# The Mamba-2 mixer of a two-layer trunk: silu by tanh, decays group by group, and an order kept on four engines

## The chip, the cores and the metric

The kernel runs on one core of a Trainium2 chip. The metric is device microseconds of one execution. TensorE is called PE in the profile, VectorE DVE, ScalarE ACT, GpSimd POOL and SyncE SP.

## The reference

A trunk of two layers works on x, 256 tokens of width 1024, in float32. Each layer adds half a SwiGLU FFN, a token mixer, a cross-attention into 256 memory tokens and another half FFN, each behind an rmsnorm. Layer 0's mixer is a differential attention; layer 1's, which this change is about, is a Mamba-2 SSD mixer with 8 groups of 4 heads, state 128 and chunks of 128 tokens:

```
z, xbc, dt = jnp.split(h @ w_in, ...)
xbc = silu(causal_depthwise_conv(xbc, conv_w, conv_b))       # 4 taps
xs, Bm, Cm = jnp.split(xbc, ...)
dt = softplus(dt + dt_bias)
y = ssd_chunked_scan(xs * dt, dt * -exp(A_log), Bm, Cm)
#   cb = C B^T;  decay = exp(a_cs[l] - a_cs[s]), lower triangle
#   y_diag = (cb * decay) x;  states = B^T (decay_to_end x);  y_off = exp(a_cs) C state
y = (y + D_skip * xs) * silu(z)
y = rmsnorm over each group of 256, * gnorm
out = y @ w_out
```

## The kernel before

**Products.** Every weight is loaded by SP into one of four 1 MB tiles (L161) and cut into *granules* of 128x1024. A granule is split into a rounded part `whi`, cast by ACT (L183), and a remainder `wlo`, subtracted by DVE (L184); four pairs of such tiles exist (pool `hp`). Each product is three matmuls, hi by hi, hi by lo and lo by hi (`mm3`, L221 to L223). `use` (L197) asks, when a granule comes up, for the splits up to `AHEAD` = 2 granules beyond it.

**Order.** The work is a list of units, each some granules and a function. `Pipe` (L108 to L140) keeps a time that advances with the matmuls emitted; a step given to `pipe.after(us, f)` is emitted when that time is reached, so the numbers in such calls set the order in which instructions are written. `run_units` (L202) then decides which engines keep that order: in the mixer only TensorE does, and a scheduler orders the other engines.

**The mixer** (`ssd`, L901). After the key and value products for the memory tokens (`mk`) and the unit `zdt` (the first half of z's first pair, and dt), `sums` makes the cumulative sums `acs` and `out_of_psum` writes them to a DRAM tile `scr`. `spread(g)` loads them back for group g, broadcast over the partitions, as tiles `E`, one per chunk (L997); `decay` turns such a tile into differences with four relus on ACT (L1011) and `decay2` into decays with one exp per chunk (L1015). Four pairs of groups follow, each with units b, c, xs (two) and z. The channels b, c and xs go through `conv`: a first tap on ACT (L1026), three taps on DVE for each half j (L1033), and silu with the bias on ACT, one 128x256 half at a time (L1038). z goes through silu on ACT straight from PSUM (L1081). For each group, TensorE then turns b (`tb`, L1087) and multiplies c by b (`pcb`, L1092); ACT copies `bn` (L1096); DVE masks `pcb` into `cbm` (L1098) and multiplies it into the two `E` tiles (L1100). TensorE turns xs (`tx`, L1107), ACT copies it (`xn`, L1111), and GpSimd makes `xd`, `xe` and the skip part `xn` (L1115 to L1119). TensorE computes the state (`pst`, L1128), the diagonal part (`py`, L1133) and the part from the first chunk's state (`pof`, L1147); DVE adds and gates (`y`, L1140 to L1156, with `yo`); ACT sums the squares (L1161) and scales (L1165), DVE prepares `msq` (L313); TensorE turns y (`ty`, L1176), and ACT and DVE split it into `y_hi` and `y_lo` (L306, L308). After the last pair the 16 granules of `out` follow.

Of the kernel before, what the change touches and what calls it, by code (L numbers as in the profile page):

```python
# [7 lines left out]
F32 = mybir.dt.float32  # L8
# [15 lines left out]
AHEAD = 2  # L24
# [33 lines left out]
def trunk(ctx, tc, a, out):  # L58
# [129 lines left out]
    done = [0]  # L188

# [6 lines left out]
    def use(gr):  # L196

        for g in gr:
            ready(g.at + AHEAD + 1)
            yield g  # L200

    def run_units():  # L202
# [698 lines left out]
    def ssd(norm, nxt, kv):  # L901
# [8 lines left out]
        dte = const.tile([P, 32], F32, name="dte")  # L910
        E = {}
# [29 lines left out]
        def dt_steps(pd):  # L941
# [15 lines left out]
            def third():  # L957
# [9 lines left out]
                v.scalar_tensor_tensor(av, dt, -1.0, nega.unsqueeze(1).broadcast_to(d32), op0=ALU.mult, op1=ALU.mult)  # L967
                pipe.after(5.0, sums)
            pipe.after(1.0, second)

        def sums():
# [9 lines left out]
            def out_of_psum():  # L981
# [35 lines left out]
        def conv(ps, ch, name, wait):  # L1017
# [18 lines left out]
            def silu():  # L1036
                for j in range(2):
                    nc.scalar.activation(o[:, j, :], o[:, j, :], AF.Silu, bias=cb_[:, ch[j]:ch[j] + 1])  # L1038
# [26 lines left out]
        def group(g):  # L1065
# [3 lines left out]
            def xs_fin(ps):  # L1069
                s["xs"] = conv(ps, (2 * g, 2 * g + 1), "xs", 6.5)  # L1070
                if g == 0:
                    s["zs"] = held.pop()
                    pipe.after(6.5, lambda: nc.scalar.activation(s["zs"], s["zs"], AF.Silu))
                pipe.after(9.5, turn_x)

            def z_fin(ps):
                zs = v2(slot("zs"))

                def go():
                    for t in range(2):  # L1080
                        nc.scalar.activation(zs[:, t, :], ps[t], AF.Silu)  # L1081
# [3 lines left out]
            def cross():  # L1085
# [8 lines left out]
                def go():  # L1094
                    s["bn"] = work("bn", P)
                    nc.scalar.copy(s["bn"], tb[:, 0:P])  # L1096
                    cbm = work("cbm", S).rearrange("p (c l) -> p c l", c=2)
                    v.tensor_tensor(cbm, pcb[:, 0:2, :], triu.unsqueeze(1).broadcast_to([P, 2, P]), op=ALU.mult)  # L1098
# [4 lines left out]
            def turn_x():  # L1103
# [5 lines left out]
                def go():  # L1109
# [34 lines left out]
            def state():  # L1144
# [7 lines left out]
                def gate():  # L1152
                    yo = work("yo", S)
                    v.tensor_tensor(r4(yo), r4(pof), b4(eacs[:, hs]), op=ALU.mult)
# [13 lines left out]
                pipe.after(evac + 7.0, lambda: rc.append(rpow(ss[:, 0:2], 1.0 / 256, 2, "yrc")))  # L1168
# [26 lines left out]
        for i in range(4):  # L1195
# [161 lines left out]
```

## Time and profile before

| | before |
|---|---|
| median of 3 runs | 1319.79 us (1319.79 to 1320.98) |
| profiled execution | 1322.33 us, span 1320.6 us |
| granted TensorE clock, mean | 0.994 |
| HBM read | 229.77 MB, 175 GB/s over the span |
| TensorE chain share of the span | 88% |

A page of the profile gives busy times by engine, the chain of work that ended last, and the costliest groups of instructions, named by the line and by output <- input. The trace behind it answers questions on windows of time, on what an engine waited for, and on the single instructions.

### The profile page before, as it was taken

How to read it: one execution, taken by the hardware profiler on the slowest of the kernel's cores; microseconds unless marked ns; L12 is line 12 of the kernel's file. 1: busy time of each engine (PE TensorE's matmuls, PEld its weight loads, DVE VectorE, ACT ScalarE, POOL GpSimd, SP SyncE). 2: the span in 40 equal slices, each digit the busy share in tenths (PEclk: the TensorE clock that was granted, in tenths of full speed). 3: DMA queues.
4: the chain of work that ended last, by engine and by line, in shares of the span. 5: the costliest groups of instructions: out<-in, count | busy, mean ns of one | idle time of the engine just before them, and what ended most of it. 6: DMA issues, size and time to landing. Idle time of an engine off the chain costs nothing.

```text
span 1320.6 us, 17832 instructions
## 1 busy us (share of the span) xinstructions
PE 1302.2 (99%) x6995; PEld 1118.0 (85%) x6995; DVE 808.7 (61%) x1178; ACT 739.8 (56%) x1208; POOL 65.2 (5%) x68
## 2 busy tenths in 40 slices
PE   9999999999999999999999999989999999999998
PEld 6888888788988888888888889889998898888887
DVE  5655457876666555555556456657985775655554
ACT  6456444585455544444445446899765664644532
POOL 1000002200000000000000000022311000000000
PEclk9999999999999999999999999889999999999999
DMA  8565555435445554656555546743544444555651
GB/s 303 191 223 173 194 178 189 129 127 166 163 150 162 190 190 128 231 184 203 181 190 186 183 156 219 222 158 128 163 157 159 160 160 157 189 181 175 207 176 49
DMA packets 134631, 232.02 MB, mean 176 GB/s; under 512 B 5737, under 2 KB 34066, under 8 KB 134546
## 3 DMA queue, kind: packets, MB, share of 16 engines
q1 hardware_dynamic: 133648, 229.75, 52.7%
q8 instruction: 55, 0.90, 0.3%
q10 hardware_dynamic: 738, 0.59, 0.1%
q0 software_dynamic: 160, 0.52, 0.1%
q14 instruction: 30, 0.25, 0.0%
HBM read 229.77 MB, written 1.08 MB: 175 GB/s over the span
## 4 chain that ended last, share of the span: by engine, by line
PE 88%; ACT 6%; DVE 2%; DMA 2%; issue 1%; POOL 1%; SPq 0%; POOLq 0%; ACTq 0%; DVEq 0%
PE out L221 7%; PE out L223 7%; PE out L222 7%; PE up L222 5%; PE up L223 5%; PE up L221 5%; PE gate L223 5%; PE gate L221 5%; PE gate L222 5%; PE htp L603 1%; PE fin L222 1%; PE fin L221 1%; PE fin L223 1%; ACT whi L183 1%; PE xq L222 1%
## 5 line engine op out<-in xcount | busy, mean ns | idle before, releaser
L184 DVE TENSOR_TENSOR wlo<-w,whi 128x1024 fp32r<-128x1024 f32 (+2 forms) x446 | 523.9, 1180 | 416.9 <-ACT whi L183 415.2
L183 ACT CAST whi<-w 128x1024 fp32r<-128x1024 f32 (+1 forms) x448 | 448.1, 1007 | 467.2 <-PE out L223 146.6
L222 PE MATMUL up<-wlo,xh 128*128 128x512 f32 x320 | 124.7, 390 | 1.1 <-DVE wlo L184 1.1
L221 PE MATMUL up<-whi,xh 128*128 128x512 f32 x320 | 124.6, 389 | 0.0
L223 PE MATMUL up<-whi,xl 128*128 128x512 f32 x320 | 124.5, 389 | 0.0
L221 PE MATMUL gate<-whi,xh 128*128 128x512 f32 x312 | 123.2, 395 | 0.0
L223 PE MATMUL gate<-whi,xl 128*128 128x512 f32 x312 | 121.6, 390 | 0.0
L222 PE MATMUL gate<-wlo,xh 128*128 128x512 f32 x312 | 121.5, 389 | 0.0
L221 PE MATMUL out<-whi,hid_hi 128*128 128x512 f32 x264 | 103.5, 392 | 0.0
L223 PE MATMUL out<-whi,hid_lo 128*128 128x512 f32 x264 | 102.8, 389 | 0.0
L222 PE MATMUL out<-wlo,hid_hi 128*128 128x512 f32 x264 | 102.7, 389 | 0.0
L222 PEld LDWEIGHTS up<-wlo,xh 128*128 128x128 f32 x320 | 60.1, 188 | 14.3 <-DVE wlo L184 1.9
L221 PEld LDWEIGHTS up<-whi,xh 128*128 128x128 f32 x320 | 60.1, 188 | 12.8 <-ACT whi L183 0.4
L223 PEld LDWEIGHTS up<-whi,xl 128*128 128x128 f32 x320 | 60.1, 188 | 12.4
L223 PEld LDWEIGHTS gate<-whi,xl 128*128 128x128 f32 x312 | 58.5, 188 | 12.3
L221 PEld LDWEIGHTS gate<-whi,xh 128*128 128x128 f32 x312 | 58.6, 188 | 11.5
L222 PEld LDWEIGHTS gate<-wlo,xh 128*128 128x128 f32 x312 | 58.6, 188 | 11.5
L223 PEld LDWEIGHTS out<-whi,hid_lo 128*128 128x128 f32 x264 | 49.6, 188 | 10.4
L222 PEld LDWEIGHTS out<-wlo,hid_hi 128*128 128x128 f32 x264 | 49.6, 188 | 10.1
L221 PEld LDWEIGHTS out<-whi,hid_hi 128*128 128x128 f32 x264 | 49.6, 188 | 9.9
L315 POOL TENSOR_TENSOR rcol<-msq,neghalf 128x2 f32<-128x2 f32 x8 | 5.6, 697 | 691.2 <-DVE msq L313 691.2
L221 PE MATMUL xs<-xh,whi 128*128 128x256 f32 x128 | 38.0, 297 | 0.2 <-ACT whi L183 0.2
(354 smaller groups left out, 2741.7 us busy)
## 6 DMA issues: line engine op xcount, KB each, us to landing
w<-in_ffn_w_up_dram SPq DMA_DIRECT2D x40, 1024.0 KB, 5.1
w<-in_ffn_w_down_dram SPq DMA_DIRECT2D x40, 1024.0 KB, 5.1
w<-in_ffn_w_gate_dram SPq DMA_DIRECT2D x38, 1024.0 KB, 5.1
w<-in_ssd_w_in_dram SPq DMA_DIRECT2D x24, 1024.0 KB, 5.2
w<-in_xa_w_kv_dram SPq DMA_DIRECT2D x16, 1024.0 KB, 4.9
w<-in_da_w_in_dram SPq DMA_DIRECT2D x12, 1024.0 KB, 5.1
w<-in_xa_w_q_dram SPq DMA_DIRECT2D x8, 1024.0 KB, 5.0
w<-in_xa_w_o_dram SPq DMA_DIRECT2D x8, 1024.0 KB, 4.9
```

The source lines that it names most:

```text
L183: nc.scalar.copy(hv, src)
L184: self.eng.tensor_tensor(self.lo[:, :, o:o + n], src, hv.bitcast(F32), op=ALU.subtract)
L221: nc.tensor.matmul(o, lhsT=lh, rhs=rh, start=start, stop=False)
L222: nc.tensor.matmul(o, lhsT=lh, rhs=rl, start=False, stop=False)
L223: nc.tensor.matmul(o, lhsT=ll, rhs=rh, start=False, stop=stop)
L315: nc.gpsimd.tensor_tensor(c[:, :n], m[:, :n], neghalf[:, :n], op=ALU.pow)
L603: nc.tensor.transpose(tp[:, j, t * P:(t + 1) * P], us[t][:, (i + j) * P:(i + j + 1) * P], ident)
```

## The change

Six things change, all in the mixer.

1. `run_units` keeps the written order on TensorE, DVE, ACT and GpSimd (SP is still ordered by the scheduler), and splits run three granules ahead.
2. silu becomes tanh: ACT computes th = tanh(v/2) in one step of 128x512, DVE computes (th + 1) v, twice the silu. The conv bias moves into the first tap. For z two tanh of 128x256 from PSUM and two steps on DVE take the place of two silus. The factors of one half are put into dt, the skip weights, `bn`, `cbm`, `yo` and the eps of the norm.
3. Loads and decays get times group by group, for groups 0 to 3 too.
4. `crosses` of a pair are written 18 us apart (6 in the last pair).
5. The two xs units of a pair become projections of their own, and the second goes behind z; in the last pair both stay ahead of z. Their weights come as 8x256 loads.
6. `inner` is written only once `bn` exists.

```diff
-        with tc.manual_schedule(engines={E.PE}):
+        with tc.manual_schedule(engines={E.PE, E.DVE, E.Activation, E.Pool}):
+            ahead[0] = AHEAD_KEPT
...
-                    pipe.after(0.5 if g < 4 else 24.0 + 7.0 * (g - 4), lambda g=g: spread(g))
+                    at = (9.0, 36.0, 47.0, 64.5, 80.5, 98.0, 114.0, 120.0)[g]
+                    pipe.after(max(0.5, at - 16.0), lambda g=g: spread(g))
                     for c in range(2):
-                        i = 2 * g + c
-                        pipe.after(6.0 + 1.3 * i if g < 4 else 33.0 + 4.0 * (i - 8), lambda g=g, c=c: decay(g, c))
-                    pipe.after((14.0, 16.0, 33.5, 36.0, 67.5, 70.0, 72.5, 75.0)[g], lambda g=g: decay2(g))
+                        pipe.after(max(6.0, at - 4.5) + 1.5 * c, lambda g=g, c=c: decay(g, c))
+                    pipe.after(at, lambda g=g: decay2(g))
...
-                    nc.scalar.activation(o[:, j, :], ps[:, j, :], AF.Copy, scale=tap(3, j))
+                    nc.scalar.activation(o[:, j, :], ps[:, j, :], AF.Identity, scale=tap(3, j),
+                                         bias=cb_[:, ch[j]:ch[j] + 1])
...
-            def silu():
-                for j in range(2):
-                    nc.scalar.activation(o[:, j, :], o[:, j, :], AF.Silu, bias=cb_[:, ch[j]:ch[j] + 1])
             pipe.after(evac, taps)
-            pipe.after(wait, silu)
+            pipe.after(wait, lambda: silu2(o, o, o, v))
             return o
+
+        def silu2(dst, src, keep, eng):
+
+            th = work("th")
+            if isinstance(src, list):
+                for t in range(2):
+                    nc.scalar.activation(th[:, t * S:(t + 1) * S], src[t], AF.Tanh, scale=0.5)
+                for t in range(2):
+                    v.scalar_tensor_tensor(dst[:, t, :], th[:, t * S:(t + 1) * S], 1.0, src[t], op0=ALU.add, op1=ALU.mult)
+            else:
+                th = v2(th)
+                nc.scalar.activation(th, src, AF.Tanh, scale=0.5)
+                eng.scalar_tensor_tensor(dst, th, 1.0, keep, op0=ALU.add, op1=ALU.mult)
...
-                t = conv(ps, (ch, ch + 1), which, 12.3 if which == "b" else 6.7)
+                t = conv(ps, (ch, ch + 1), which, 6.5)
...
-                        pipe.after(10.0 + 2.5 * j, crosses[g])
+                        pipe.after(10.0 + (6.0 if i == 3 else 18.0) * j, crosses[g])
...
-                    nc.scalar.copy(s["bn"], tb[:, 0:P])
+                    nc.scalar.mul(s["bn"], tb[:, 0:P], 0.5)
...
-                    v.tensor_tensor(cbm, pcb[:, 0:2, :], triu.unsqueeze(1).broadcast_to([P, 2, P]), op=ALU.mult)
+                    v.scalar_tensor_tensor(cbm, pcb[:, 0:2, :], 0.25, triu.unsqueeze(1).broadcast_to([P, 2, P]),
+                                           op0=ALU.mult, op1=ALU.mult)
...
-                    pipe.after(8.5, inner)
+                    pipe.when(8.5, lambda: "bn" in s, inner)
...
-            proj("a", w_in, 2048 + 512 * i, 512, norm, "xs", fx)
+            def xs(j):
+                proj("a", w_in, 2048 + 512 * i + 256 * j, 256, norm, "xs", [fx[j]])
+            xs(0)
+            if i == 3:
+                xs(1)
             if i == 0:
                 proj("b", w_in, 256, 256, norm, "z", [lambda ps, f=fz[1]: f([ps[:, t, :] for t in range(2)])])
             else:
                 wide([(w_in, 512 * i, 512)], norm, "z",
                      lambda ps, fz=fz: [f([p[:, j * 256:(j + 1) * 256] for p in ps]) for j, f in enumerate(fz)])
+            if i < 3:
+                xs(1)
```

How the order changes is shown at three places. A row is the line, the operation, output <- input and shape, and x is how often it stands there in a row. First SP's queue at the start of pair 0; `scr` are the cumulative sums, `E` the decay tiles, `w` weight tiles. Before:

```order
L161 DMA w<-in_ssd_w_in_dram 128x8x256
L987 DMA scr<-acst 32x256
L997 DMA E<-scr 128x4x128 x8
L161 DMA w<-in_ssd_w_in_dram 128x8x256 x2
L161 DMA w<-in_ssd_w_in_dram 128x4x512
L997 DMA E<-scr 128x4x128 x2
```

And after, from xs's first weights on:

```order
L161 DMA w<-in_ssd_w_in_dram 128x8x256 x5
L994 DMA scr<-acst 32x256
L161 DMA w<-in_ssd_w_in_dram 128x8x256
L1004 DMA E<-scr 128x4x128 x2
L161 DMA w<-in_ssd_w_in_dram 128x8x256 x2
L1004 DMA E<-scr 128x4x128 x2
L161 DMA w<-in_ssd_w_in_dram 128x4x512 x2
```

The E loads of groups 0 to 3 stood together behind scr, ahead of pair 1's first weights (b); now that weight load stands ahead of group 0's two, and the other groups' loads come between later weights.

Second ACT, from the end of mk to the silu of pair 0's b; `whi` are casts, `E<-E,acs` relus, `E<-E` exps, `b<-b` and `c<-c` first taps. Before:

```order
L183 CAST whi<-w 128x1024 x2
L1011 ACTIVATE E<-E,acs 128x128 x11
L813 COPY mk<-mk 128x512
L1026 ACTIVATE b<-b,cols_112 128x256 x2
L1011 ACTIVATE E<-E,acs 128x128
L183 CAST whi<-w 128x1024
L1011 ACTIVATE E<-E,acs 128x128 x8
L183 CAST whi<-w 128x1024
L1011 ACTIVATE E<-E,acs 128x128 x4
L1026 ACTIVATE c<-c,cols_112 128x256 x2
L1011 ACTIVATE E<-E,acs 128x128 x4
L1015 ACTIVATE E<-E 128x512 x2
```

And after, where `th` is a tanh:

```order
L183 CAST whi<-w 128x1024
L1018 ACTIVATE E<-E,acs 128x128 x4
L183 CAST whi<-w 128x1024
L1018 ACTIVATE E<-E,acs 128x128 x4
L1033 ACTIVATE b<-b,cols_111,cols_112 128x256 x2
L1022 ACTIVATE E<-E 128x512 x2
L183 CAST whi<-w 128x1024 x2
L1058 ACTIVATE th<-b 128x512
L1033 ACTIVATE c<-c,cols_111,cols_112 128x256 x2
L183 CAST whi<-w 128x1024 x2
L1058 ACTIVATE th<-c 128x512
```

Before, 28 relus stood there, and the silu of b came later still; now only group 0's eight relus do, the first four of them ahead of xs's second cast, and b's tanh follows the two exps.

Third DVE in pair 1, from the taps of group 2's xs to its E; `wlo` are splits. Before:

```order
L184 TENSOR_TENSOR wlo<-w,whi 128x1024
L1033 SCALAR_TENSOR_TENSOR xs<-xs,cols_112 128x253
L1033 SCALAR_TENSOR_TENSOR xs<-xs,cols_112 128x255
L1154 TENSOR_TENSOR yo<-pof,eacs 128x256
L1033 SCALAR_TENSOR_TENSOR xs<-xs,cols_112 128x254
L1155 TENSOR_TENSOR y<-y,yo 128x256
L1033 SCALAR_TENSOR_TENSOR xs<-xs,cols_112 128x253
L1156 TENSOR_TENSOR y<-y,zs 128x512
L184 TENSOR_TENSOR wlo<-w,whi 128x1024
L1098 TENSOR_TENSOR cbm<-pcb,cst 128x256
L1033 SCALAR_TENSOR_TENSOR xs<-xs,cols_112 128x255
L1100 TENSOR_TENSOR E<-E,cbm 128x512 x2
```

And after:

```order
L184 TENSOR_TENSOR wlo<-w,whi 128x1024
L1041 SCALAR_TENSOR_TENSOR xs<-xs,cols_112 128x255
L1041 SCALAR_TENSOR_TENSOR xs<-xs,cols_112 128x254
L1041 SCALAR_TENSOR_TENSOR xs<-xs,cols_112 128x253
L184 TENSOR_TENSOR wlo<-w,whi 128x1024
L1157 TENSOR_TENSOR y<-py,xn 128x512
L316 TENSOR_SCALAR msq<-yss 128x2
L1114 SCALAR_TENSOR_TENSOR cbm<-pcb,cst 128x256
L1117 TENSOR_TENSOR E<-E,cbm 128x512 x2
L1059 SCALAR_TENSOR_TENSOR xs<-th,xs 128x512
L184 TENSOR_TENSOR wlo<-w,whi 128x1024
```

The taps of xs are no longer mixed with the gating, and group 2's new step `xs<-th,xs` stands behind the split, y, msq, cbm and both E, in an order that is kept.

More of the change, by code (lines that the diff above doesn't have):

```diff
@@ L22 @@
 EPS = 1e-6
-AHEAD = 2
+AHEAD, AHEAD_KEPT = 2, 3
 T = dict(gate=5.5, hid=3.0, turn=1.3, row=5.0, rot=5.5, probs=(1.0, 4.0, 7.0, 10.0), tp=8.5, heads=4.5, otp=6.5,
@@ L188, in trunk @@
     done = [0]
+    ahead = [AHEAD]
     def ready(n):
@@ L198, in use @@
         for g in gr:
-            ready(g.at + AHEAD + 1)
+            ready(g.at + ahead[0] + 1)
             yield g
@@ L213, in run_units @@
             f(*gs)
-        with tc.manual_schedule(engines={E.PE}):
+        with tc.manual_schedule(engines={E.PE, E.DVE, E.Activation, E.Pool}):
+            ahead[0] = AHEAD_KEPT
             for gs, f in units[written[0]:written[1]]:
                 f(*gs)
+            ahead[0] = AHEAD
         for gs, f in units[written[1]:]:
@@ L308, in split_act, with rpow @@
             nc.vector.scalar_tensor_tensor(l_, s_, c_, h_.bitcast(F32), op0=ALU.mult, op1=ALU.subtract)
-    def rpow(src, scale, n, name):
+    def rpow(src, scale, n, name, eps=EPS):
         m = sm.tile([P, 16], F32, name="msq", tag="msq")
-        nc.vector.tensor_scalar(m[:, :n], src, scale, EPS, op0=ALU.mult, op1=ALU.add)
+        nc.vector.tensor_scalar(m[:, :n], src, scale, eps, op0=ALU.mult, op1=ALU.add)
         c = sm.tile([P, 16], F32, name=name, tag=name)
@@ L910, in ssd @@
         dte = const.tile([P, 32], F32, name="dte")
+        dskh = const.tile([P, 32], F32, name="dskh")
         E = {}
@@ L967, in third @@
                 v.scalar_tensor_tensor(av, dt, -1.0, nega.unsqueeze(1).broadcast_to(d32), op0=ALU.mult, op1=ALU.mult)
+                v.tensor_scalar(dt, dt, 0.5, None, op0=ALU.mult)
+                v.tensor_scalar(dskh, dsk, 0.5, None, op0=ALU.mult)
                 pipe.after(5.0, sums)
@@ L1072, in xs_fin @@
                     s["zs"] = held.pop()
-                    pipe.after(6.5, lambda: nc.scalar.activation(s["zs"], s["zs"], AF.Silu))
+                    pipe.after(1.0, lambda: silu2(s["zs"], s["zs"], s["zs"], v))
                 pipe.after(9.5, turn_x)
@@ L1079, in go @@
                 def go():
-                    for t in range(2):
-                        nc.scalar.activation(zs[:, t, :], ps[t], AF.Silu)
+                    silu2(zs, ps, None, v)
                     s["zs"] = zs
@@ L1119, in go @@
                     nc.gpsimd.tensor_tensor(xn.rearrange(r24, r=4), xn.rearrange(r24, r=4),
-                                            dsk[:, hs].unsqueeze(1).unsqueeze(3).broadcast_to(bh), op=ALU.mult)
+                                            dskh[:, hs].unsqueeze(1).unsqueeze(3).broadcast_to(bh), op=ALU.mult)
                     s.update(xn=xn, xd=xd, xe=xe)
-                    pipe.after(8.5, inner)
+                    pipe.when(8.5, lambda: "bn" in s, inner)
                 pipe.after(evac, go)
@@ L1153, in gate @@
                     yo = work("yo", S)
-                    v.tensor_tensor(r4(yo), r4(pof), b4(eacs[:, hs]), op=ALU.mult)
+                    v.scalar_tensor_tensor(r4(yo), r4(pof), 0.5, b4(eacs[:, hs]), op0=ALU.mult, op1=ALU.mult)
                     v.tensor_tensor(y[:, 1, :], y[:, 1, :], yo, op=ALU.add)
@@ L1167, in state @@
                 pipe.after(evac + 4.5, square)
-                pipe.after(evac + 7.0, lambda: rc.append(rpow(ss[:, 0:2], 1.0 / 256, 2, "yrc")))
+                pipe.after(evac + 7.0, lambda: rc.append(rpow(ss[:, 0:2], 1.0 / 256, 2, "yrc", 4 * EPS)))
                 pipe.after(evac + 10.0, scale)
```

## The prediction

> **What bounds the kernel now.** I read the page first, then the busy time by stage of the mixer, then the waits of TensorE there. The page says which engine sets the time:
>
> ```profile
> PE 1302.2 (99%) x6995; PEld 1118.0 (85%) x6995; DVE 808.7 (61%) x1178; ACT 739.8 (56%) x1208; POOL 65.2 (5%) x68
> ```
>
> TensorE is busy 99% of the span, and the change leaves its set of matmuls as it is. So a gain can only come from time in which it stood still or ran at a lower clock. The windows of the mixer's stages (columns: window, length, busy PE, PEld, DVE, ACT, POOL, granted clock, DMA share) say where that is:
>
> ```profile
> 822.40:859.60 37.20, 34.34 (x257) 33.21 (x256) 23.76 (x38) 31.43 (x70) 0.59 (x1) 0.91 0.70 216
> 859.60:909.00 49.40, 44.63 (x308) 41.93 (x307) 33.87 (x56) 45.84 (x93) 11.52 (x11) 0.93 0.46 142
> 952.15:994.40 42.25, 42.25 (x307) 39.78 (x306) 34.17 (x57) 27.56 (x55) 9.65 (x9) 1.00 0.45 154
> ```
>
> Pair 3, the last row, is 42.25 us of TensorE without a hole. Pair 1, the middle row, has the same kind of work and takes 49.40: it loses 7.15. Pair 0, the first row, loses 37.20 - 34.34 = 2.86 to idle time and more to the clock. Four windows of 5 us show that clock:
>
> ```profile
> 845.00:850.00 5.00, 3.59 (x18) 3.09 (x17) 2.45 (x4) 4.99 (x9) 0.00 (x0) 0.67 0.95 305
> 850.00:855.00 5.00, 5.00 (x32) 5.00 (x31) 5.00 (x10) 3.15 (x7) 0.00 (x0) 0.65 0.63 195
> 865.00:870.00 5.00, 1.07 (x5) 1.08 (x6) 2.05 (x3) 4.94 (x6) 0.00 (x0) 0.71 0.68 215
> 870.00:875.00 5.00, 5.00 (x30) 5.00 (x29) 1.48 (x4) 4.99 (x13) 2.65 (x3) 0.60 0.33 100
> ```
>
> The first two rows miss (0.33 + 0.35) x 5 = 3.40 us of clock, the last two (0.29 + 0.40) x 5 = 3.45: two stretches that each cost 3.4. Pair 0 loses 2.86 + 3.40 = 6.26, both pairs 13.4. That is the most that this change can give back: 1.0% of the span.
>
> TensorE's own waits between 795 and 1010 us (in total, times, longest) name what it stood for, and ACT's rows there what kept ACT:
>
> ```profile
> PE tx L1107 <- ACT xs L1038: 5.5, 3, 4.8
> PE tb L1087 <- ACT b L1038: 1.1, 1, 1.1
> PE xs L223 <- DVE wlo L184: 0.8, 1, 0.8
> ```
>
> ```profile
> L1015 ACT ACTIVATE E<-E 128x512 f32<-128x512 f32 x16 | 9.7, 634 | 0.1
> L1038 ACT ACTIVATE xs<-xs,cols 128x256 f32<-128x256 f32 x16 | 8.1, 505 | 2.4 <-DVE xs L1033 2.4
> L1015 ACT ACT_TABLE_LOAD x6 | 7.7, 1283 | 0.1
> ```
>
> It waits for silu on ACT, which is full in those windows (4.94 to 4.99 of 5), and a silu next to an exp pays a table load of 1.283.
>
> **The change, part by part.** *Tanh for silu.* The table loads of the mixer, six of them in the row above, fall from 14 to 1 in the order: 13 x 1.283 = 16.7 us off ACT. Thirty-two silus of 0.505 (sixteen of xs in the row, as many of b and c) become sixteen tanh of 128x512, of about the exp's 0.634: 16.2 against 10.1. So ACT sheds some 22 us in pairs 0 and 1 above all, where it was the late engine. VectorE gets the rest of the silu: 17 steps on 128x512 and 14 on 128x256. Steps are best read from start to start:
>
> ```profile
> 893.25 0.41 DVE L1154 TENSOR_TENSOR yo<-pof,eacs 128x256 f32<-128x256 f32 x1
> 893.58 0.47 DVE L1033 SCALAR_TENSOR_TENSOR xs<-xs,cols 128x254 f32<-128x254 f32 x1
> 893.97 0.42 DVE L1155 TENSOR_TENSOR y<-y,yo 128x256 f32<-128x256 f32 x1
> ...
> 894.69 0.68 DVE L1156 TENSOR_TENSOR y<-y,zs 128x512 f32<-128x512 f32 x1
> 895.29 1.22 DVE L184 TENSOR_TENSOR wlo<-w,whi 128x1024 fp32r<-128x1024 f32 x1
> 896.42 0.42 DVE L1098 TENSOR_TENSOR cbm<-pcb,cst 128x256 f32<-128x256 f32 x1
> ```
>
> A 128x256 step takes 0.33, a tap 0.39, a 128x512 step 0.60, a split (wlo) 1.13. The added steps are 4 x 0.60 + 4 x 0.33 = 3.7 us per pair. No row shows the new step on 128x512 itself; it lies between 0.60 (the product of that size) and 0.78 (two taps), and I take 0.60 as the nearest. VectorE then has 34.17 + 3.7 = 38 of 42.25: it still fits, but with little room, and now in an order that it may not change.
>
> *Kept order, three granules ahead.* There are four pairs of hi and lo tiles, so a split three granules ahead writes into the tiles that TensorE read last. In the order of VectorE shown with the change, the split ahead of cbm, E and the new xs step therefore can't start before TensorE has left that granule, and all that stands behind it waits too. TensorE's pace, from its rows:
>
> ```profile
> 876.55 0.60 PE L1128 MATMUL pst<-xe,bn 128*128 128x256 f32 x2
> 878.69 0.36 PE L221 MATMUL c<-xh,whi 128*128 128x256 f32 x1
> 878.89 0.28 PE L222 MATMUL c<-xl,whi 128*128 128x256 f32 x1
> 879.01 0.28 PE L223 MATMUL c<-xh,wlo 128*128 128x256 f32 x1
> 940.12 0.27 PE L1087 MATMUL tb<-ident,b 128*128 128x128 f32 x1
> 940.59 0.48 PE L221 MATMUL z<-whi,xh 128*128 128x512 f32 x1
> 940.91 0.39 PE L222 MATMUL z<-wlo,xh 128*128 128x512 f32 x1
> 941.14 0.40 PE L223 MATMUL z<-whi,xl 128*128 128x512 f32 x1
> ```
>
> That is 0.12 for a matmul of 256 columns, 0.23 for one of 512, 2.1 for pst with py, 0.47 for tb with pcb; tx, ty, pof I take at 0.3 each by the rows' durations (0.27 for a tb of the same shape). ACT's steps come from these:
>
> ```profile
> 826.91 1.28 ACT L1011 ACTIVATE E<-E,acs 128x128 f32<-128x128 f32 x4 [0.46 <-DMA E<-scr]
> ...
> 839.64 1.16 ACT L1015 ACTIVATE E<-E 128x512 f32<-128x512 f32 x2
> 840.68 1.29 ACT L1011 ACTIVATE E<-E,acs 128x128 f32<-128x128 f32 x4
> 841.85 1.06 ACT L183 CAST whi<-w 128x1024 fp32r<-128x1024 f32 x1
> 842.78 1.18 ACT L1015 ACTIVATE E<-E 128x512 f32<-128x512 f32 x2
> ```
>
> Four relus take 1.17, two exps 1.04, a cast 0.93 to the next start and 1.06 to its end.
>
> Now tx of group 2 (pair 1). The split's tile is free once 24 matmuls of z are done; then cast 1.06, split 1.13, y 0.60, msq 0.1, cbm 0.33, two E 1.20, the xs step 0.60: 5.0 us. TensorE has 18 matmuls of z (4.1) and a pof (0.3) before tx: 4.4. Wait 0.6. In pair 2 a ty more stands there: wait 0.3. In pair 3 both xs units come before z. From the end of the second on, cast and split 2.2, cbm, E, xs step 2.13, y_lo 0.8, three taps 1.17, split 1.13, taps 1.17, yo and two y 1.26, split 1.13, cbm, E, xs step 2.13: 13.1 until group 7 may be turned; TensorE has 42 matmuls of z (9.7), 0.9 for ty, pof and tx, and 0.47: 11.1. Wait 2.0; group 6 by the same count is ready at 4.3 with its tx due at 4.7.
>
> *Decays group by group.* SyncE's queue sets when the first decays arrive:
>
> ```profile
> 821.43 0.35 SPq L987 DMA_DIRECT2D scr<-acst  x1
> 823.45 6.15 SPq L997 DMA_DIRECT2D E<-scr  x8
> DMA to landing us min/median/max: 3.4/5.3/5.7
> ```
>
> Before, the E loads followed scr at once, and the first landed 3.4 later, where ACT waited for it (826.91). After, pair 1's first weight load stands between, and it needs the tile of c: TensorE leaves mk at 822.40, so that c's second cast ends at 823.5, its split at 824.7; E then issues half a microsecond behind that load (an issue takes 0.35 by scr's row), at 825.2, and with the median of 5.3 lands at 830.5. In ACT's order its relu stands ahead of xs's second cast, and the chain goes on from there: relu and cast 832.6, relu 833.8, two taps of b 834.5 (0.7, an estimate from relus of half their width at 0.29 each), exps 835.6, z's cast 836.6, its split 837.8, three taps of b 839.0, split 840.1, b step 840.7, taps of c 841.9, split 843.0, taps 844.2, split 845.3, c step 845.9. TensorE gets to pcb after 180 matmuls: 822.40 + 21.6 = 844.0. Wait 2.0. Behind it zs 0.6, taps and splits of xs 4.6, cbm, E and the xs step 2.13 put tx of group 0 at 853.2, against 845.9 + 0.36 + 48 x 0.12 = 852.0: wait 1.2. Had the loads landed at the minimum, 3.4 after an issue at 823.4, the chain would end 3.7 earlier and both waits would be gone; those are the two ends for this part, 0 and 3.2.
>
> *The second xs behind z* moves matmuls within the pair and is in those counts. *The factors of one half* ride in steps that exist, but for two of about 0.2 us on VectorE while TensorE computes mk. *Narrower weight loads* move the same bytes. If that cover went, they would cost what they take: 0.4 us.
>
> The sum of the waits: 2.0 + 1.2 + 0.6 + 0.3 + 2.0 = 6.1. *The clock:* before the first stretch TensorE had idled 1.1 for b, 0.8 for a split and little else, so a wait of 2.0 is as much as set it off. A stretch costs 3.4; in pair 0 it also lets the others catch up and swallows the 1.2 behind, net 2.2. I count it there. For pair 3's equal wait, which rests on a longer chain, I leave it to a rival. The loss is 8.3 against 13.4: a gain of 5.1. The profiled execution took 1322.3 (the span of 1320.6 and 1.7 around it), so it would come to 1317.2; its working stands 2.5 above the median of 1319.8, and from that I forecast 1314.7.
>
> The Trainium skill's page "TensorE: Matmul & The Clock Gate" (section "HAM oscillation — how this bites in real kernels") gives as its abstract rule that only idle gaps longer than about 3.4 us bring the slow clock. This trace disagrees at its first stretch, which came with no wait above 1.1.
>
> **The rivals.** *A, every wait goes:* the loads land early and three granules ahead cover the rest. All 13.4 come back: 1306.4. For it: ACT's 22 us. Against it: the counts for pairs 1 to 3, which don't hang on the loads. *B, the gain is eaten:* pair 3's wait takes a stretch as well, 3.4 more: loss 11.7, time 1318.1, not to be told from no change, since runs of this kernel tell about 0.2% (2.6 us). *C, waits of two microseconds leave the clock alone:* loss 6.1 without a stretch, 1312.5. For it: 2.0 is close to what was needed before. The rule of the Trainium skill named above would give this time as well. *D, slower:* VectorE becomes the bound, because in kept order nothing can pass a split that is late. GpSimd's work slows a split:
>
> ```profile
> 902.95 1.68 DVE L184 TENSOR_TENSOR wlo<-w,whi 128x1024 fp32r<-128x1024 f32 x1
> ```
>
> ```profile
> 903.63 1.47 POOL L1118 TENSOR_TENSOR xe<-xd,dte 128x256 f32<-128x256 f32 x1
> ```
>
> Beside GpSimd's xe the split takes 0.46 more than the 1.22 of the one at 895.29. One such split, and one split more to pass (1.13), ahead of each of the five waits adds 1.6 to each: 6.1 + 8.0 = 14.1, and with waits of 2 and more three stretches follow, 3 x 2.2: loss 20.7, time 1327.1. It decides from 1.5 us of added lag on. Against it: VectorE has 4 us to spare per pair, spread over five such places.
>
> **How the numbers follow.** Forecast 0.40, A 0.17, B 0.17, C 0.09, D 0.17. Faster: 0.36 of the forecast, A and C, 0.62; the same: B and 0.03 of the forecast, 0.20; slower: D and the last 0.01, 0.18. The range reaches down to A's 1306.4, the other end of the unknown landing, and up to 1322, which leaves out most of D.
>
> **What would show it.** Right: ACT's table loads nearly gone; no wait for silu of xs from ACT, but short waits of tx and pcb for VectorE's xs and c steps; a wait of about 2 at pcb in pair 0 and at group 7's tx; at most one stretch of half clock; pairs 1 and 2 at about 43. The row of E's first landing (near 830) tells the forecast from A. Wrong: a loss in pairs 1 to 3 of more than 2 us each, or VectorE idle where I have it late.

## The result and the profile after

The change makes the kernel slower: 1328.04 us median (1327.28 to 1328.80, 4 runs) against 1319.79 (1319.31 to 1320.98), a ratio of 1.006 with a 95% interval of 1.0046 to 1.0073. The forecast was 1314.7 with a range of 1306.4 to 1322.0. The profiled execution took 1327.69 us, with a span of 1325.9.

First the windows of the mixer's stages, from the first matmul of each pair's b to the next (same columns as before; the last row ends with the first matmul of out):

```profile
821.64:858.01 36.37, 32.46 (x252) 32.23 (x251) 24.92 (x38) 19.82 (x36) 0.00 (x0) 0.91 0.66 203
858.01:902.46 44.45, 42.20 (x305) 39.34 (x304) 37.85 (x60) 31.54 (x67) 11.15 (x10) 1.00 0.52 160
902.46:946.29 43.83, 42.39 (x309) 39.74 (x308) 38.75 (x64) 32.70 (x72) 9.01 (x8) 1.00 0.53 163
946.29:999.71 53.42, 47.48 (x318) 43.07 (x317) 45.24 (x71) 35.84 (x81) 9.50 (x8) 0.94 0.46 149
```

Pair 1 took 49.40 before and takes 44.45: 5 us are won there, and 0.8 in pair 0. Pair 3 took 42.25 without a hole and takes 53.42: 11.2 are lost. ACT is relieved (pair 1: 45.84 busy before, 31.54 now); VectorE is now the fuller helper, 45.24 in pair 3 against 34.17. The gain worked out for pair 0 came (0.9, measured 0.8), that for pair 1 in most part (6.6, measured 5.0), and in pair 3 a loss of 11.2 came where 2.0 was worked out. TensorE's waits in the mixer, and ACT's table loads there:

```profile
PE tx L1124 <- DVE xs L1059: 8.8, 4, 3.1
PE pcb L1108 <- DVE c L1059: 4.1, 2, 3.9
PE z L224 <- ACT state L1155: 0.7, 1, 0.7
```

```profile
L955 ACT ACT_TABLE_LOAD x1 | 1.3, 1283 | 0.0
```

Before, TensorE waited for silu on ACT; now nearly all its waits are for the new steps on VectorE. One load of a table is left of 14. Windows of 5 us in pair 3 show what two of these waits bring:

```profile
980.00:985.00 5.00, 2.84 (x13) 1.91 (x12) 4.93 (x9) 3.77 (x8) 0.00 (x0) 1.00 0.25 49
985.00:990.00 5.00, 5.00 (x20) 4.18 (x21) 4.82 (x11) 1.26 (x2) 0.00 (x0) 0.66 0.41 161
990.00:995.00 5.00, 3.18 (x15) 2.29 (x13) 4.93 (x6) 2.83 (x8) 3.97 (x3) 1.00 0.07 3
995.00:1000.00 5.00, 3.71 (x12) 3.17 (x13) 2.28 (x3) 0.11 (x1) 0.00 (x0) 0.66 0.56 210
```

TensorE idles, and a stretch at 0.66 of the clock follows, twice; VectorE is busy 4.8 to 4.9 of 5 in the three windows up to 995. This is rival D's picture, at its price (1327.1): waits of 12.7 us in all at tx and at pair 0's pcb (14.1 in D) and three stretches of half clock, two of them in pair 3.

Pair 0 followed the chain of the prediction. SyncE's queue and ACT's first steps:

```profile
821.49 0.35 SPq L994 DMA_DIRECT2D scr<-acst  x1
824.08 0.38 SPq L161 DMA_DIRECT2D w<-in_ssd_w_in_dram  x1
825.85 0.92 SPq L1004 DMA_DIRECT2D E<-scr  x2
```

```profile
830.89 1.28 ACT L1018 ACTIVATE E<-E,acs 128x128 f32<-128x128 f32 x4 [5.22 <-DMA E<-scr]
...
972.53 0.63 ACT L1058 ACTIVATE th<-c 128x512 f32<-128x512 f32 x1 [1.59 <-DVE c L1041]
973.06 1.27 ACT L1018 ACTIVATE E<-E,acs 128x128 f32<-128x128 f32 x4
974.23 1.00 ACT L1033 ACTIVATE xs<-xs,cols,cols 128x256 f32<-128x256 f32 x2
975.13 1.27 ACT L1018 ACTIVATE E<-E,acs 128x128 f32<-128x128 f32 x4
976.30 0.90 ACT L1182 ACTIVATE y<-y,yrc 128x256 f32<-128x256 f32 x2
977.10 1.04 ACT L183 CAST whi<-w 128x1024 fp32r<-128x1024 f32 x1
...
979.36 1.04 ACT L183 CAST whi<-w 128x1024 fp32r<-128x1024 f32 x1
```

The weight load went ahead of the decays, which let ACT go on 9.2 us after the pair's start (8.1 was worked out), and pcb waited 3.9 us (2.0 was). The rows from 972.53 on are pair 3, read together with VectorE's:

```profile
835.23 1.52 DVE L1041 SCALAR_TENSOR_TENSOR b<-b,cols 128x255 f32<-128x255 f32 x3 [0.87 <-ACT b L1033]
...
846.66 0.68 DVE L1059 SCALAR_TENSOR_TENSOR c<-th,c 128x512 f32<-128x512 f32 x1
...
946.38 1.23 DVE L184 TENSOR_TENSOR wlo<-w,whi 128x1024 fp32r<-128x1024 f32 x1 [1.68 <-ACT whi L183]
949.31 1.23 DVE L184 TENSOR_TENSOR wlo<-w,whi 128x1024 fp32r<-128x1024 f32 x1 [1.70 <-ACT whi L183]
...
951.26 1.52 DVE L1041 SCALAR_TENSOR_TENSOR xs<-xs,cols 128x255 f32<-128x255 f32 x3 [0.65 <-ACT xs L1033]
...
953.83 1.51 DVE L1041 SCALAR_TENSOR_TENSOR xs<-xs,cols 128x255 f32<-128x255 f32 x3
...
960.04 1.51 DVE L1041 SCALAR_TENSOR_TENSOR b<-b,cols 128x255 f32<-128x255 f32 x3
961.47 1.21 DVE L184 TENSOR_TENSOR wlo<-w,whi 128x1024 fp32r<-128x1024 f32 x1
...
973.61 0.68 DVE L1059 SCALAR_TENSOR_TENSOR c<-th,c 128x512 f32<-128x512 f32 x1
975.27 1.52 DVE L1041 SCALAR_TENSOR_TENSOR xs<-xs,cols 128x255 f32<-128x255 f32 x3 [0.97 <-ACT xs L1033]
978.17 1.23 DVE L184 TENSOR_TENSOR wlo<-w,whi 128x1024 fp32r<-128x1024 f32 x1 [1.39 <-ACT whi L183]
...
990.42 1.52 DVE L1173 TENSOR_TENSOR y<-y,zs 128x512 f32<-128x512 f32 x1
991.87 1.63 DVE L184 TENSOR_TENSOR wlo<-w,whi 128x1024 fp32r<-128x1024 f32 x1
...
995.47 0.68 DVE L1059 SCALAR_TENSOR_TENSOR xs<-th,xs 128x512 f32<-128x512 f32 x1
```

And TensorE's rows there, among them the ends of b and of the last xs (the rows behind them) and its longest waits:

```profile
847.40 1.01 PE L1108 MATMUL pcb<-c,b 128*128 128x128 f32 x3 [3.91 <-DVE c L1059]
...
954.24 0.27 PE L1103 MATMUL tb<-ident,b 128*128 128x128 f32 x1
...
976.34 0.40 PE L224 MATMUL z<-whi,xh 128*128 128x512 f32 x1
...
984.88 0.66 PE L1124 MATMUL tx<-ident,xs 128*128 128x128 f32 x4 [2.16 <-DVE xs L1059]
...
996.29 1.09 PE L1124 MATMUL tx<-ident,xs 128*128 128x128 f32 x4 [3.12 <-DVE xs L1059]
```

VectorE stands for casts of ACT around the start of pair 3, 1.68 and 1.70. The taps at 951.26 and 953.83 are those of pair 2's second xs, which now stands behind z: VectorE works off three xs units in pair 3 (18 taps of xs), where it has two (12 taps) in pairs 1 and 2, and two in pair 3 before the change. TensorE is through with pair 3's b at 954.2; VectorE gets to b's first tap at 960.04, 5.8 us later (2.4 before the change, at 962.46). Pair 2 was entered just as late, 6.0 (910.40 to 916.36), and took 43.8 us all the same; in pair 3 the lag feeds itself: c's taps are late, so ACT waits 1.59 for them before c's tanh; behind that tanh stand group 7's relus, the taps of xs and a scaling, and only then the cast, at 977.10; and now VectorE, though late, stands idle for ACT twice, 0.97 and 1.39. Each engine waits for the other in turn, in an order that neither may change.

### The profile page after: what moved, and what is told of

The parts are those of the page before. It is cut to its first block, busy times and chain, and to the rows that moved or that the text cites. A ratio compares the mean times of both kernels' runs of the same rounds, so it can differ in the third digit from the quotient of the medians.

```text
span 1325.9 us, 17826 instructions
## 1 busy us (share of the span) xinstructions
PE 1301.7 (98%) x6995; PEld 1117.2 (84%) x6995; DVE 830.4 (63%) x1211; ACT 714.5 (54%) x1176; POOL 65.8 (5%) x68
## 4 chain that ended last, share of the span: by engine, by line
PE 85%; DVE 8%; ACT 2%; DMA 2%; issue 2%; POOL 0%; POOLq 0%; SPq 0%; ACTq 0%; DVEq 0%
PE out L224 7%; PE out L226 7%; PE out L225 7%; PE up L225 5%; PE up L226 5%; PE up L224 5%; PE gate L226 5%; PE gate L224 5%; PE gate L225 5%; DVE wlo L184 3%; PE htp L606 1%; PE fin L224 1%; PE fin L225 1%; PE fin L226 1%; PE xq L225 1%
## 5 line engine op out<-in xcount | busy, mean ns | idle before, releaser
L224 PEld LDWEIGHTS gate<-whi,xh 128*128 128x128 f32 x312 | 58.7, 188 | 11.4
L224 PE MATMUL fin<-whi,hid_hi 128*128 128x512 f32 (+1 forms) x110 | 38.3, 348 | 0.0
```

The lines of the kernel that those rows point to most:

```text
L224: nc.tensor.matmul(o, lhsT=lh, rhs=rh, start=start, stop=False)
```

## Experiments

The theory (lag): VectorE's work in a fixed order fills nearly all of TensorE's time per pair, lag is carried on, and pair 3, with both xs units ahead of z, has no time to absorb it. Rivals: the tile pairs (three ahead), the place of xs, ACT's order, tanh itself, the loads. All times below are medians; each kernel is compared with the kernel before on its own chip (1319.7 to 1320.5).

**Splits two ahead.**

```diff
-AHEAD, AHEAD_KEPT = 2, 3
+AHEAD, AHEAD_KEPT = 2, 2
```

> The changed kernel (1328.0 us) with splits two granules ahead in the mixer, as before, instead of three. Theory lag (VectorE enters pair 3 late because its work, kept in one order, fills 38.75 of 43.80 us in pair 2, and both xs units ahead of z then leave it no time): VectorE's work is the same, so pair 3 still takes over 50 us (53.4 in the changed kernel) and the time is 1325 to 1331. Rival buffers (a split three ahead needs the tile pair that TensorE has just left, so that VectorE and ACT stand waiting for TensorE with everything behind them): pair 3 falls below 47 us and the time to 1321 or less.

1321.91 us (ratio 1.0016, 1.0007 to 1.0025). The pairs take 34.3, 41.7, 42.9 and 51.2 us. Both theories had a part of it: 6 us come back, most in pairs 0 and 1, but pair 3 keeps 9 of its 11. In pair 1 TensorE no longer waits at all.

**The last xs behind z.**

```diff
-            if i == 3:
-                xs(1)
...
-            if i < 3:
-                xs(1)
+            xs(1)
```

> The changed kernel with the second xs of pair 3 behind z, as in the other three pairs. Theory lag: part of pair 3's 11 us stays, since VectorE still comes in about 5 us late; tx of group 6 still waits 2 us or more, pair 3 takes 46 to 49 us, the time is 1321 to 1325. Rival order (the place of this one unit is the whole cause): pair 3 takes 44 us like pairs 1 and 2, the time is 1318.5 to 1320. If neither the lag nor the place matters, pair 3 stays over 52.

1327.03 us (1.0064, 1.0047 to 1.0081). Pair 3 falls to 46.2, inside what the lag theory said, but the time hardly moves. The windows of pair 3 and of out tell why:

```profile
947.61:993.83 46.22, 43.40 (x312) 40.17 (x311) 41.25 (x67) 33.87 (x77) 9.65 (x8) 1.00 0.50 164
993.83:1044.95 51.12, 48.89 (x232) 40.17 (x231) 31.83 (x47) 28.35 (x53) 6.39 (x6) 0.97 0.44 149
```

Out takes 51.1 us where the changed kernel takes 46.3: group 7 is now finished so late that TensorE waits 1.6 us for its ty and 0.6 for y_hi in out, both from ACT, where the changed kernel has no wait in out. The loss was only moved.

**The first decays early.**

```diff
-                        nc.sync.dma_start(E[g, c], scr[...].partition_broadcast(P))
+                        (nc.gpsimd if g == 0 else nc.sync).dma_start(E[g, c], scr[...].partition_broadcast(P))
```

> The changed kernel with the two decay loads of group 0 issued from GpSimd's queue, so that they no longer stand behind pair 1's weight load. The step of the prediction for pair 0: E lands before 829 (830.9 in the changed kernel), the 5.2 us that ACT waited for it shrinks to under 3, the wait of pcb for the c step (3.9 us) falls below 1, and the time falls by 3 to 5 us, to 1323 to 1325; pair 3 stays at 52 to 54. If another chain is nearly as late in pair 0, the wait of pcb stays above 2 and the time within 2 us of 1328.

1329.57 us (1.0079, 1.0064 to 1.0094). This one missed its aim: GpSimd issued the loads 5.9 us after the pair's start, where SyncE had issued them 4.2 after it, and ACT waited 5.7 us instead of 5.2:

```profile
828.16 1.70 POOL L1004 DMA_DIRECT2D E<-scr  x2 [34.40 <-PE b L225]
```

It says nothing on what early loads are worth by themselves.

**Silu on ACT.** Factors of one half are taken out with it.

```diff
-                nc.scalar.activation(th, src, AF.Tanh, scale=0.5)
-                eng.scalar_tensor_tensor(dst, th, 1.0, keep, op0=ALU.add, op1=ALU.mult)
+                nc.scalar.activation(dst, src, AF.Silu)
```

> The changed kernel with silu on ACT again in one step and without the factors of one half, everything else as changed; VectorE loses the 31 added steps (3.7 us per pair), ACT gets its table loads back. Theory lag: VectorE no longer comes late into pair 3, which falls to 43 to 46 us, and what ACT gets back (14 loads of 1.28) costs less than that: 1317 to 1323. Rival ACT (ACT's kept order, with decays of groups 6 and 7 ahead of casts, is what is late in pair 3): more work on ACT makes pair 3 longer than 53 us and pair 1 longer than 46: 1330 or more.

1320.72 us (1.0007, 0.9998 to 1.0016); pairs 36.6, 41.7, 44.2 and 47.3. Giving ACT back some 20 us of work and taking 15 from VectorE wins 7 us, so the rival falls as it was put; pair 3 stays 1.3 over what the lag theory said. Pair 1 shows one thing more:

```profile
860.00:901.80 41.80, 41.80 (x305) 39.50 (x304) 34.73 (x53) 37.58 (x73) 11.83 (x10) 1.00 0.59 176
```

It has no hole left although silu and its table loads are back on ACT. The gain in pair 1, which the prediction drew from ACT's relief by tanh, does not need tanh.

**Both together.** The edits of two ahead and of silu on ACT.

> Splits two granules ahead (alone 1321.9 us) and silu on ACT again (alone 1320.7) together in the changed kernel. If the two costs are separate (a split that needs the tile pair TensorE has just left; VectorE's 3.7 us per pair), they add: pairs of about 34.5, 41.7, 43 and 45 us, 1314 to 1318. If they are one lag that either of them removes, the time stays at 1320 to 1322.

1315.06 us (0.996, 0.9945 to 0.9974); pairs 32.4, 41.7, 43.5 and 45.9. The two costs add.

**Tanh alone in the kernel before.** The times of the decays, the place of xs, two ahead and the scheduler are as before.

> The kernel before with silu by tanh and nothing else of the change: the scheduler orders all engines but TensorE, two granules ahead, both xs ahead of z, decays at the old times. Theory lag (tanh's steps on VectorE cost only where an order kept on all engines lets nothing pass): ACT's table loads go, pairs 0 and 1 get back 5 to 10 of the 13.4 us, 1310 to 1315. Rival tanh (VectorE's added work is too much in any order): 1319 or more, pair 3 over 45 us.

1328.53 us (1.0064, 1.0049 to 1.0079). Here the theory fell: even where the scheduler may order VectorE, tanh costs 8.5 us. It does what it is for in pair 0 (34.5 against 37.2), but pair 1 gets longer:

```profile
857.20:909.20 52.00, 45.45 (x308) 42.21 (x308) 42.46 (x72) 38.95 (x86) 14.79 (x14) 0.94 0.51 159
```

VectorE is busy 42.46 us there against 33.87 before, with 72 steps against 56: eight are tanh's, the others taps, cbm, E and splits that fall into this pair here. TensorE's waits in the mixer are mostly for its xs steps, five times, 11.4 us in all; pair 3 takes 45.8. So the added work is too much there in the scheduler's order as well.

**The last decays earlier**, with two ahead.

```diff
-                    at = (9.0, 36.0, 47.0, 64.5, 80.5, 98.0, 114.0, 120.0)[g]
+                    at = (9.0, 36.0, 47.0, 64.5, 80.5, 94.0, 103.0, 109.0)[g]
```

> Splits two granules ahead, and the decays of groups 5, 6 and 7 written at 94, 103 and 109 instead of 98, 114 and 120, so that group 7's relus leave the stretch of ACT between c's tanh and the cast. If these relus, in kept order, make the cast late and VectorE stand idle in pair 3 (1.0 and 1.4 us in the kernel with two ahead), pair 3 falls from 51.3 to 47 to 49 us and the time from 1321.9 to 1318 to 1320. If VectorE's own lag is all, pair 3 stays at 50 to 52.

1320.23 us (1.0001, 0.9992 to 1.0010); pair 3 takes 50.9. The relus ahead of the cast are a link of the chain, for VectorE's wait for that cast falls from 1.39 to 0.44; but pair 3 wins only 0.4 us by it, since VectorE is late without it too.

**The scheduler's order, two ahead.**

```diff
-        with tc.manual_schedule(engines={E.PE, E.DVE, E.Activation, E.Pool}):
+        with tc.manual_schedule(engines={E.PE}):
```

> Splits two granules ahead and the order kept on TensorE alone, as before; tanh, the decays by group and the place of xs as changed. Theory kept order (steps that are ready stand behind steps that are not): pair 3 falls from 51.3 us to 46 or less, the time to 1312 to 1317. Rival load (VectorE has too much to do in pair 3 in any order): pair 3 over 49 and the time within 2 us of 1321.9.

1316.56 us (0.9971, 0.9958 to 0.9984), faster than before; but pair 3 is still 49.3, so that it is pairs 0 and 3 (31.2 and 49.3, against 34.3 and 51.2) that gain; pair 1 stays at 41.7 and pair 2 is 0.7 longer, at 43.7. VectorE is busy 42.83 us in pair 3, again with three xs units:

```profile
938.30:987.60 49.30, 45.27 (x317) 42.00 (x316) 42.83 (x71) 33.06 (x70) 10.58 (x10) 0.95 0.47 151
```

It gets to pair 3's b 1.5 us behind TensorE here, not 5.8, so a late entry is not needed for pair 3 to be long. That VectorE's load is, the next but one shows.

**The scheduler's order, two ahead, silu on ACT.**

> Splits two granules ahead, the order kept on TensorE alone, silu on ACT: of the change only the decays by group, the place of the second xs, the times of the crosses and the bias in the first tap remain. If kept order and tanh are two costs that add, 1309 to 1313 (kept order on four engines with silu on ACT: 1315.1; scheduler with tanh: 1316.6). If ACT's table loads, which the scheduler may scatter, take it back, 1316 to 1322.

1313.01 us (0.9951, 0.9936 to 0.9966); pairs 30.5, 41.7, 42.3 and 47.0. ACT loads tables 22 times (28 us) and has room for it but in pair 3, where it is busy 45.1 of 47.0 us and TensorE waits 3.4 for silu of xs. From the 1321.9 us of two ahead, the scheduler's order alone wins 5.4, silu on ACT alone 6.9, both 8.9: the two costs overlap. Pairs 0 and 1 are 14.4 us shorter than before the change, with silu on ACT as it was. So what the change wins there comes from its other parts (decays by group, the second xs behind z, the times of the crosses, the bias in the first tap, the narrower loads), which no run takes apart.

**Tanh in pairs 0 to 2, silu in pair 3**, the scheduler's order, two ahead.

```diff
-            pipe.after(wait, lambda: silu2(o, o, o, v))
+            pipe.after(wait, lambda: silu2(o, o, o, v, one))
...
+            if one:
+                nc.scalar.activation(dst, src, AF.Silu)
+                return
```

> As the kernel with two ahead and the scheduler's order (1316.6 us), but in pair 3 silu is computed on ACT, so that VectorE loses 3.7 us there; the factors of one half hold for the other groups only. Theory lag: pair 3 falls from 49.3 to 43 to 46 us, the time to 1310 to 1314. If pair 3's loss comes from the place of xs or from ACT, it stays over 48 and the time at 1315 to 1319.

1312.18 us (0.9945, 0.9930 to 0.9960), the lowest median of all, though its interval does not tell it from the 1313.01 without any tanh. Pair 3:

```profile
939.57:983.34 43.77, 43.41 (x315) 40.62 (x315) 38.41 (x66) 34.39 (x70) 9.77 (x8) 1.00 0.44 147
```

Pair 3 falls from 49.3 to 43.8, and VectorE's busy time there from 42.83 to 38.41. Taking tanh's work off VectorE shortens pair 3 in both orders (in the kept one from 53.4 to 47.3).

**The scheduler's order, three ahead.** The changed kernel with the edit of the scheduler's order and nothing else.

> The changed kernel with the order kept on TensorE alone, and still three granules ahead. Theory buffers (three ahead costs because what stands behind a split in a kept order waits for its tiles): with the scheduler other steps pass, so that three ahead costs at most 2 us against two ahead: 1315 to 1319. Rival: three ahead costs in any order: 1321 or more.

1314.97 us (0.9963, 0.9950 to 0.9976): the kept order of the three helpers costs 13 us. Its windows, beside those of the changed kernel, show where:

```profile
826.35:857.87 31.52, 30.08 (x252) 29.88 (x252) 24.37 (x37) 23.59 (x46) 0.86 (x1) 1.00 0.69 211
857.87:899.61 41.74, 41.74 (x304) 39.43 (x304) 38.51 (x62) 32.23 (x69) 10.80 (x11) 1.00 0.54 163
899.61:941.82 42.21, 42.21 (x308) 39.82 (x308) 37.76 (x64) 32.29 (x68) 8.73 (x8) 1.00 0.53 162
941.82:987.23 45.41, 43.65 (x316) 40.65 (x316) 40.30 (x71) 34.10 (x72) 8.50 (x9) 1.00 0.53 182
```

The work per pair is the same to a count or two (60 to 62 steps of VectorE in pair 1, 64 in pair 2), the stages are 4.9, 2.7, 1.6 and 8.0 us shorter, and no half clock is left in them. (Of these 17 us some 4 are lost ahead of pair 0, where TensorE waits 1.5 us for an issue, runs at 0.51 of its clock from 824.0 to 826.3 and reaches b at 826.1; why it waits is open.) Three ahead costs nothing here: it did so only where what stands behind a split may not pass it.

**Five tile pairs** in the changed kernel.

```diff
-    hp = ctx.enter_context(tc.tile_pool(name="hp", bufs=4))
+    hp = ctx.enter_context(tc.tile_pool(name="hp", bufs=5))
...
-    sp = ctx.enter_context(tc.tile_pool(name="sp", bufs=32))
+    sp = ctx.enter_context(tc.tile_pool(name="sp", bufs=29))
```

> The changed kernel, three ahead and in kept order, with five pairs of hi and lo tiles instead of four (and 29 slots of 128x512 instead of 32 to make room). Theory buffers: a split no longer needs the tiles that TensorE has just left, so the time falls like with two ahead, by 4 to 7 us, to 1321 to 1324, pair 3 to 49 to 51.5. Rival early splits (the split itself, asked for earlier, stands ahead of more urgent steps, whatever its tiles): 1326 or more, pair 3 over 52.

1322.34 us (1.0015, 1.0005 to 1.0025), as much as two ahead gives. Pairs 0 and 1 are 34.3 and 41.7 like there: the reason given for three ahead, a split that needs the tiles TensorE has just left, is shown. Pair 3 keeps 52.8, over what was expected: the tiles are not its cause.

**Order kept on TensorE and VectorE; on TensorE and ACT.** Two kernels, each with the set of engines cut to these two.

> The changed kernel with the order kept on TensorE and VectorE, ACT and GpSimd left to the scheduler. With all four kept it takes 1328.0 us and 53.4 in pair 3, with TensorE alone 1315.0 and 45.4. Theory VectorE (its steps, in a fixed order, stand behind splits that are not ready): nearly all of the cost stays, 1324 to 1329, pair 3 over 50. Rival ACT (ACT's fixed order makes casts and tanhs late, and VectorE only follows): it goes, 1314 to 1318, pair 3 below 47. If it takes both, the cost falls by about half, 1319 to 1323.

> The changed kernel with the order kept on TensorE and ACT, VectorE and GpSimd left to the scheduler. Theory VectorE: the cost goes, 1314 to 1318, pair 3 below 47; pair 0 keeps what the first decay load costs in ACT's order (pcb waits over 2 us). Rival ACT: it stays, 1324 to 1329, pair 3 over 50. If it takes both, 1319 to 1323.

1319.78 us (1.0004, 0.9994 to 1.0013) and 1323.06 (1.0030, 1.0019 to 1.0042); pair 3 takes 47.9 and 50.3. Over the 1314.97 with neither, VectorE's kept order costs 4.8, ACT's 8.1, the two together 13.1. Both rivals held a part, and the parts add. ACT's is the larger one although ACT is the emptier engine: it is busy 36 of 53 us in pair 3. Every unit's casts, taps, tanhs and relus pass through it in one row, which may be the reason; no run shows it.

**Tanh but in pair 3, three ahead**, the scheduler's order.

> Three granules ahead, the order kept on TensorE alone, silu on ACT in pair 3 only: the two best single steps together (1315.0 with three ahead and 1312.2 with silu in pair 3, two ahead). If three ahead helps in the scheduler's order, 1309 to 1312; if pair 3 is at TensorE's pace already (43.8 with two ahead), 1311 to 1313, no more than 1312.2 can tell from.

1312.92 us (0.9949, 0.9934 to 0.9964), the same as two ahead.

**Taps by turns** in the changed kernel.

```diff
-            def others(j):
+            def others():
                 for k in (2, 1, 0):
                     d = 3 - k
-                    v.scalar_tensor_tensor(o[:, j, d:], ...)
+                    for j in range(2):
+                        v.scalar_tensor_tensor(o[:, j, d:], ...)
```

> The changed kernel with VectorE's taps of the two halves written by turns, so that no tap follows the one whose result it reads; work, order kept and three ahead as changed. In the changed kernel three taps in a row take 1.43 us to the next start, in the kernel before, mixed with other steps, 1.17. Theory lag: six taps fall from 2.86 to about 2.34, VectorE has 2.1 us less per pair, comes less late into pair 3, and the time falls to 1320 to 1325, pair 3 to 47 to 51. Rival: the end of a tap's result isn't what spaces them, or the lag comes from waits alone: six taps stay over 2.7, the time at 1326 to 1330.

1321.78 us (1.0009, 0.9999 to 1.0018): 6.3 us for writing the same steps in another order. VectorE's rows:

```profile
836.53 2.43 DVE L1041 SCALAR_TENSOR_TENSOR b<-b,cols 128x255 f32<-128x255 f32 x6 [0.86 <-ACT b L1033]
838.88 1.22 DVE L184 TENSOR_TENSOR wlo<-w,whi 128x1024 fp32r<-128x1024 f32 x1
```

Six taps take 2.35 us to the next start; in the changed kernel three of them take 961.47 - 960.04 = 1.43, six 2.86. Sixteen units make 8.2 us of VectorE, of which 6.3 show in the time; pair 3 falls to 50.0.

**Kept order mended:** taps by turns, two ahead, silu in pair 3, the order kept on four engines.

> Order kept on four engines as in the change, but two ahead, taps by turns, and silu on ACT in pair 3. If the kept order costs only through these lags, it comes to what the scheduler's order gives with the same parts (1312.2): 1311 to 1316. If a kept order costs by itself, 1317 or more.

1314.89 us (0.9959, 0.9944 to 0.9974), within what was expected, though 2.7 behind the scheduler's 1312.18, which the two intervals do not settle. Pair 3 takes 48.0 us there against 43.8; ACT is busy 44.0 of them, and TensorE's longest wait, 2.1, is for its silu of xs. So a kept order does not have to lose against the kernel before.

## Why the prediction was wrong

*Right.* The 13.4 us that could come back, and that they lie in pairs 0 and 1: the change got 5.8 of them, the scheduler's kernel with silu on ACT 14.4. The table loads (14 to 1). The decays behind the weight load. The split three ahead that waits for TensorE's tiles, if dearer than worked out: without it pairs 0 and 1 win 2.0 and 2.7. The waits were for the steps named. At pcb in pair 0 and at tx of groups 0, 2, 4, 6 and 7 they were worked out as 2.0, 1.2, 0.6, 0.3, 0 and 2.0, in all 6.1; measured were 3.9, 0, 2.1, 1.4, 2.2 and 3.1, in all 12.7.

*The step that failed* is the one that summed VectorE: "VectorE then has 34.17 + 3.7 = 38 of 42.25: it still fits, but with little room". In pairs 1 and 2 VectorE was busy 37.9 and 38.8, near that sum; in pair 3, for which it was made, 45.2. Three things were wrong in it.

First a size: a tap was taken at 0.39 from rows where taps stand between other steps. In the kept order three taps of one half stand in a row, each reading what the one ahead wrote, and take 1.43 for 1.17. That is 0.26 for each of eight such rows in a pair, 2.1 us, over half of what tanh adds, and the profile before did show it, where three taps of b stood alone:

```profile
832.19 1.52 DVE L1033 SCALAR_TENSOR_TENSOR b<-b,cols 128x255 f32<-128x255 f32 x3 [4.48 <-ACT b L1026]
833.62 1.22 DVE L184 TENSOR_TENSOR wlo<-w,whi 128x1024 fp32r<-128x1024 f32 x1
```

Pair 0's chain holds four such rows: its c step ended 25.7 us after the pair's start (23.5 worked out), 1.1 later by the landing and 1.0 by the taps.

Second, it left out an xs unit. Pair 2's second xs goes behind z, so its taps, cbm, E and xs step fall to VectorE in pair 3, about 5 us of work (2.86 for six taps, 2.13 for the rest as the prediction prices it), and pair 3's own two stand ahead of z. With pair 3's own second xs behind z as well, pair 3 takes 46.2, and out is 4.8 longer.

Third, the sum for each tx started from an engine without lag: "from the end of the second on, cast and split 2.2". In the run that cast began at 979.36, 3.0 us after the end of the second xs, and VectorE entered the pair 5.8 us late. The count of 13.1 us to the end of group 7's step came to 19.7. ACT's kept order, which the prediction priced only where decays stand ahead of a cast in pair 0, costs 8.1 us when only ACT and TensorE keep theirs.

The runs price the failed step: with tanh's steps off VectorE the changed kernel wins 7.3 us, with two ahead 6.1, with both 13.0 and comes to 1315.06. That this is the 1314.7 of the forecast is luck, since it is reached without tanh.

Rival D, with a chance of 0.17, had VectorE as the bound and came within 1 us. Its argument against itself, "VectorE has 4 us to spare per pair", is the sum that failed. Its own price was in part luck too: it added a split slowed by GpSimd and one more to pass at each wait, where the runs show taps in a row, a third xs unit and ACT's order.

*The source of the gain.* "So ACT sheds some 22 us in pairs 0 and 1 above all, where it was the late engine" was true of ACT's load (pair 1: 45.84 to 31.54), but pair 1 came to 41.7 with silu on ACT as well, and tanh alone made it longer (52.0). Only in pair 0 does tanh alone win, 2.6 us.

*Half clocks.* One stretch was counted, in pair 0. There were one in pair 0 and two in pair 3, behind waits of 3.9, 2.2 and 3.1.

What stays open: what early decays are worth by themselves in pair 0, since the kernel made for it issued them later; which part of the change wins pairs 0 and 1; and why ACT's kept order costs more than VectorE's, and what the scheduler lets pass that saves pair 3 (VectorE stands for casts at the start of that pair there too): the two kernels show the price of each order and do not take it apart.

## What to carry to other kernels

Taking work off a jammed engine is worth what it costs the engine that gets it, at the tightest stage and in the order in which it stands there: here tanh took some 20 us off ACT and cost some 3.5 us of time in the scheduler's order with two ahead and 7.3 in the changed kernel, while pairs 0 and 1 got as short without it. Moving a unit behind another also moves its work on the helpers into the next stage, so the sum has to be made for each stage anew. A fixed order on helpers needs slack in every stage, and a step that waits for a buffer that TensorE must leave first makes everything behind it wait as well. Before fixing an order, write dependent steps of one engine apart from each other, and sum up the engine's time with the price that they have in that order.

## What the runs showed of the hardware

VectorE starts a 128x255 step 0.39 us after the last when the two are independent, and 0.51 after it when it reads that step's result: six in a row take 2.35 by turns and 2.86 half after half. The Trainium skill's page "VectorE: DVE Perf Modes" (section "The DRAIN you can't avoid") says that the next step doesn't start until the pipeline is empty, and adds that one that is not held starts earlier. Both are seen here: a step that reads the result of the last, of 0.48, starts 0.03 after its end, and one that doesn't starts 0.09 before it.

VectorE's y in pair 3 took 1.52 and the split behind it 1.63, against 0.68 and 1.22 in the kernel before (at 894.69 and 895.29), while GpSimd was at work:

```profile
990.35 1.04 POOL L1132 TENSOR_TENSOR xd<-xn,dt 128x512 f32<-128x512 f32 x1 [16.10 <-ACT xn L1128]
991.47 0.94 POOL L1135 TENSOR_TENSOR xe<-xd,dte 128x256 f32<-128x256 f32 x1
992.38 2.02 POOL L1136 TENSOR_TENSOR xn<-xn,dskh 128x512 f32<-128x512 f32 x1
```

That agrees with the Trainium skill's page "SBUF — State Buffer" (section "SBUF: two separate sides"), which has the two engines share a pair of ports that one holds for a whole instruction. It adds about 1.2 us at the worst place of this kernel.

A wait of TensorE of 2.2 us, at 984.88, was followed by a granted clock of 0.66 over the next 5 us. The rule of the Trainium skill's page "TensorE: Matmul & The Clock Gate" (section "HAM oscillation — how this bites in real kernels"), which the prediction cites, would have left the clock alone there; this is the second place of this case that speaks against it. The length of a wait does not decide it by itself: one of 1.5 us in the scheduler's kernel with three ahead was followed by 0.51 (824.0 to 826.3), and one of 2.1 in the changed kernel's pair 1, at 894.39, by no drop (1.00 to the end of the pair).
